# Position-table loads moved into the first block, and the first stage's seven-product block moved from fifth place to fourth

## The chip, the cores and the metric

The kernel runs on one core of one Trainium2 chip. The metric is the device time of one execution in microseconds (us), as the median of several runs. A profiled execution has, beside its time, a span: the stretch that the profiler's records cover.

## The reference

Two layers of a hybrid trunk work on one sequence of 256 tokens with 1024 channels, all in float32; a last RMSNorm follows. In each layer:

```
h = h + 1/2 * SwiGLU_a(RMSNorm(h))     # "ffn1": 1024 -> 2 x 2816 -> 1024
u = RMSNorm(h);  z = u @ W_in          # mixing: three causal branches (two attentions, one pooling)
h = h + m @ W_out
h = h + 1/2 * SwiGLU_b(RMSNorm(h))     # "ffn2", as ffn1

def swiglu(x, w_gate, w_up, w_down):
    return (silu(x @ w_gate) * (x @ w_up)) @ w_down
```

The attention branches need tables made from the input `positions` (256 integers): cosine and sine of rotary angles, and the negative distance between any two positions, masked causally. The differential attention also needs a scalar per layer worked out from the input `lamrow` (products, sums, exponentials). All of these are made once and used from the first mixing stage on.

## The kernel before

**Products.** Every float32 product is made of three matmuls on fp32r operands: a number is split into `hi`, a cast, and `lo`, the number less its cast, and `mm3` (L211 to L214) adds hi·hi (L212), lo·hi (L213, with the `lo` of the weights) and hi·lo (L214). Weights are split on the fly: a load on SyncE's queue (SP) brings a `raw` tile of 512 columns by 4 x 128 rows (1 MB; 6 buffers), ScalarE (ACT) casts `hi` (L194), VectorE (DVE) subtracts `lo` (L195); `hi` and `lo` have 3 buffers each. The first six tiles are loaded and split in four pieces of 128x512 (L200; 24 pieces of 256 KB in all).

**The opening.** After each of these pieces the list `opening` (filled at the end of the program, L1046 to L1052) gives up one callback. The callbacks load and split the columns of the transposed input, `u.first(k)` (L447 to L453: `uhi`, `ulo`), and then load the four quarters of `h`.

**A feed-forward stage**, `ffn` (L493 to L585), goes over the hidden width in blocks of 512 columns: c = 0, 512, 1024, 1536, 2048 and a last one of 256. A block makes the gate product (m=0) and the up product (m=1), each of two weight tiles and 48 matmuls. The results go through Silu (`sg`, ACT, L568) and a multiplication (`g`, DVE, L570). The `g` of a block is transposed during the next one, by `turned` (8 transposes, L503; split into `ghi` and `glo`, L486 and L487), behind the m=0 product or inside it. Block c=0 makes its four sums side by side. After each block `ahead` (L176) splits the next weight tile in advance.

**The seven-product block.** One block of a stage (`Seven`, L226 to L316) does its two products in seven half-size ones instead of eight. It needs prepared operands: `stream` (L236) makes sums and differences of the activations (`uf`, L240; `sf`, L245; `sh`, L249; `sl`, L250) two blocks ahead, and `sums` (L252) and `more` load the block's weight tiles (L161) and make differences of them (`t1`, `t2` and others, L258) one block ahead. Which block it is stands in `sevens` (L35 to L37): c=2048, the fifth, in layer 0's ffn1, and c=1536, the fourth, in the other three stages. The down projection (`Down`, L318 to L391) has similar preparations, made in block 2048, or in the last block where block 2048 is the seven-product one.

**The tables.** `tables` (L601 to L668) is called at the start of block c=512 of the first stage through `midway` (L515). It loads the positions twice, `pi` (two per partition, L607) and `pr` (all 256 to every partition, L608), and `lamrow` as `lr` (L658). All three loads are on ACT's queue. Before `pi` and `pr` stand copies on GpSimd (POOL) that write a bit of the block's `g` into the tiles, so that the loads don't start earlier. DVE then makes integer parts (`ci`, `ri`, L616), their floats (`cf`, `rf`, L618), distances (`part`, `ndist`, L620 to L625) and angles; ACT makes sines (L650 to L653) and exponentials (L663).

**What sets the order.** Each engine takes its instructions in order. The order on an engine is that of a scheduler working on the program as it is written; the times in the trace follow from semaphore waits. All loads on the two hardware queues share eight semaphores, DMAHW0 to DMAHW7, in rotation: a load waits until the load before it on its semaphore has landed.

Of the kernel before, what the change touches and what calls it, by code (L numbers as in the profile page):

```python
# [11 lines left out]
F32 = mybir.dt.float32  # L12
F32R = mybir.dt.float32r
I32 = mybir.dt.int32
# [5 lines left out]
P = 128  # L20
D = 1024
S = 256
DEPTH = 2
DFF = 2816
EPS = 1e-6
KD = D // P
# [5 lines left out]
NEG = -1e30  # L32


def sevens(layer, pre):  # L35

    return (2048,) if (layer, pre) == (0, "ffn1") else (1536,)  # L37

# [11 lines left out]
def plan():  # L52

    tiles = []

    def add(name, layer, k, nk, c, nc_):
        tiles.append((name, layer, k, nk, c, nc_))

    def ffn(layer, pre):
        for c in range(0, 2 * DFF, 1024):  # L60
            blocks = range(c, min(c + 1024, 2 * DFF), 512)
            order = [(b, k) for k in (0, 4) for b in blocks] if c == 0 else [(b, k) for b in blocks for k in (0, 4)]
            if c // 2 in sevens(layer, pre):
                order = [(c, 0), (c + 512, 0), (c + 512, 4), (c, 4)]
            for b, k in order:
                add(f"{pre}_gu", layer, k, 4, b, 512)
        for half in range(2):
            for k in range(0, KF, 4):
                add(f"{pre}_w_down", layer, k, min(4, KF - k), half * 512, 512)

    for l in range(DEPTH):
        ffn(l, "ffn1")
        for c, n in ((C_CQ, 416), (C_P, 512), (C_DQ, 512)):
            for k in (0, 4):
                add("w_in", l, k, 4, c, n)
        add("mla_w_uq", l, 0, 2, 0, 768)
        add("ukv", l, 0, 1, 0, 1024)
        for c in (C_DK, C_DV):
            for k in (0, 4):
                add("w_in", l, k, 4, c, 512)  # L80
        add("pool", l, 0, 4, 0, 128)
        for half in range(2):
            for i in range(3):
                for k in (0, 4):
                    add("w_in", l, k, 4, C_G + i * D + half * 512, 512)
        for half in range(2):
            for i in (2, 0, 1):
                add(f"w_branch{i}", l, 0, 4, half * 512, 512)
        for half in range(2):
            for k in (0, 4):  # L90
                add("w_out", l, k, 4, half * 512, 512)
        ffn(l, "ffn2")
    return tiles
# [3 lines left out]
def trunk(ctx, tc, x, xt, positions, wall, small, lamrow, fnorm, out):  # L97
    nc = tc.nc
# [8 lines left out]
    tp = ctx.enter_context(tc.tile_pool(name="tp", bufs=2))  # L107
    sp = ctx.enter_context(tc.tile_pool(name="sp", bufs=4))
# [10 lines left out]
    def big(shape, dt, name):  # L119
        return s8.tile(shape, dt, tag="s8", name=name, bufs=7)  # L120
# [44 lines left out]
    opening = []  # L165
# [4 lines left out]
    def wsplit(spec):  # L170

        if spec not in pending_splits:
            pending_splits[spec] = wsplit_now(spec)
        return pending_splits.pop(spec)
# [36 lines left out]
    def mm3(ps, lh, ll, rh, rl, start, stop):  # L211
        nc.tensor.matmul(ps, lhsT=lh, rhs=rh, start=start, stop=False)  # L212
        nc.tensor.matmul(ps, lhsT=lh, rhs=rl, start=False, stop=False)  # L213
        nc.tensor.matmul(ps, lhsT=ll, rhs=rh, start=False, stop=stop)  # L214
# [278 lines left out]
    def ffn(l, pre, u, following, midway=None):  # L493
        ghi, glo = [], []
# [18 lines left out]
        for c in range(0, DFF, 512):  # L513
            n = min(512, DFF - c)
            if c == 512 and midway:  # L515
                midway(g[0][:, :2])
            spec = lambda b, k: (f"{pre}_gu", l, k, 4, b, 512)
            if c == 0:

                ps = [[b() for _ in range(2)] for b in (acc, trp)]  # L520
                for k0 in (0, 4):
                    for m in range(2):
                        wh, wl = wsplit(spec(m * 512, k0))
                        for k in range(4):
                            for t in range(2):
                                tk = slice(t * P, (t + 1) * P)
                                mm3(ps[m][t], u.xh(k0 + k)[:, tk], u.xl(k0 + k)[:, tk], wh[:, k, :], wl[:, k, :],
                                    k0 + k == 0, k0 + k == KD - 1)
                if opened:
                    u.squares(0)  # L530
                    u.squares(1)
                u.factor()
                seven = Seven(u.xh, u.xl)
                down = Down(lambda k: ghi[0][:, k, :], lambda k: glo[0][:, k, :])
            elif c in sevens(l, pre):
                rows = seven.run(lambda: turned(*pending))
                ps = [[rows[t][m] for t in range(2)] for m in range(2)]
            elif n == 512:
                ps = []
                if c + 512 in sevens(l, pre):  # L540
                    at = 2 * c + 1024
                    last = latest[0]
                    seven.sums([spec(at, 0), spec(at + 512, 0), spec(at + 512, 4), spec(at, 4)])
                    latest[0] = last
                for m in range(2):
                    ps.append(gemm_tokens([spec(2 * c + m * 512, k) for k in (0, 4)], u.xh, u.xl, 512))
                    if m == 0:
                        turned(*pending)
                        if c + 1024 == sevens(l, pre)[0]:
                            seven.stream(u.hi, u.lo)  # L550
                        elif c == 2048 and c not in sevens(l, pre):
                            down.stream(ghi[0], glo[0], big)
            else:
                if not down.sh:
                    down.stream(ghi[0], glo[0], big)
                both = gemm_tokens([spec(2 * c, k) for k in (0, 4)], u.xh, u.xl, 512, lambda: turned(*pending))
                ps = [[b[:, m * n:(m + 1) * n] for b in both] for m in range(2)]
            if c + 512 in sevens(l, pre):
                seven.more()
            elif n < 512:  # L560
                down.open(lambda half, k: (f"{pre}_w_down", l, k, min(4, KF - k), half * 512, 512))
            elif c not in sevens(l, pre):
                ahead()
            g = []
            for t in range(2):
                r = u.r[:, t:t + 1]
                sg = tp.tile([P, n], F32, tag="B", name="sg")
                nc.scalar.activation(out=sg, in_=ps[0][t], func=AF.Silu, scale=r)  # L568
                gt = tp.tile([P, n], F32, tag="A", name="g", bufs=4)
                nc.vector.scalar_tensor_tensor(out=gt, in0=ps[1][t], scalar=r, in1=sg, op0=ALU.mult, op1=ALU.mult)  # L570
                g.append(gt)
            pending = c, g
# [25 lines left out]
    groups = [(0, range(p, NH, 2), P) for p in range(2)]  # L598
    groups += [(1, range(p + 4 * j, p + 4 * j + 4, 2), S) for j in range(2) for p in range(2)]

    def tables(after):  # L601
        pi = sp.tile([P, 2], I32, tag="pi", name="pi", bufs=1)
        pr = tp.tile([P, S], I32, tag="C", name="pr")

        nc.gpsimd.tensor_copy(out=pi, in_=after.bitcast(I32))
        nc.gpsimd.tensor_copy(out=pr[:, :2], in_=after.bitcast(I32))
        nc.scalar.dma_start(out=pi, in_=positions.rearrange("b (t p) -> (b p) t", p=P))  # L607
        nc.scalar.dma_start(out=pr, in_=positions.broadcast_to([P, S]))  # L608

        part = big([P, 2, 2, S], F32, "part")  # L610
        ci = sp.tile([P, 2, 2], I32, tag="ci", name="ci", bufs=1)
        cf = sp.tile([P, 2, 2], F32, tag="cf", name="cf", bufs=1)
        ri = tp.tile([P, 2, S], I32, tag="C", name="ri")
# [30 lines left out]
        for bits in (5, 13, 21, 40):  # L644
            c = math.floor(rest * 2.0 ** bits) / 2.0 ** bits if bits < 40 else rest
# [8 lines left out]
        nc.vector.tensor_scalar(out=sinq, in0=sink, scalar1=MLA_SCALE, scalar2=None, op0=ALU.mult)  # L654
        nc.vector.tensor_scalar(out=cosq, in0=cosk, scalar1=MLA_SCALE, scalar2=None, op0=ALU.mult)

        lr = tp.tile([P, DEPTH, 4, 32], F32, tag="C", name="lr")
        nc.scalar.dma_start(out=lr.rearrange("p l f d -> p (l f d)"), in_=lamrow.broadcast_to([P, DEPTH * P]))  # L658
        lpr = tp.tile([P, DEPTH, 2, 32], F32, tag="C", name="lpr")
        nc.vector.tensor_tensor(out=lpr, in0=lr[:, :, 0::2, :], in1=lr[:, :, 1::2, :], op=ALU.mult)  # L660
        le = sp.tile([P, DEPTH, 2], F32, tag="le", name="le", bufs=1)
# [360 lines left out]
    def last_half(n):  # L1022
# [8 lines left out]
        for t in range(2):  # L1031
# [4 lines left out]
            if n == 0:  # L1036
# [9 lines left out]
    u = Norm(0, SM_F1)  # L1046
    u.first(0)
    opening += [lambda: None] * 2 + [lambda: u.first(1), lambda: (u.first(2), u.first(3))]
    opening += [lambda k=k: u.first(k) for k in range(4, KD)] + [lambda: None] * 4
    opening += [lambda t=t, n=n: nc.sync.dma_start(out=h[:, t, n * 512:(n + 1) * 512],  # L1050
                                                   in_=x[t * P:(t + 1) * P, n * 512:(n + 1) * 512])
                for n in range(2) for t in range(2)]  # L1052
    for l in range(DEPTH):
        u = ffn(l, "ffn1", u, lambda: Norm(l, SM_MX), tables if l == 0 else None)
        u = mixing(l, u, lambda: Norm(l, SM_F2))
        u = ffn(l, "ffn2", u, (lambda: Norm(l + 1, SM_F1)) if l + 1 < DEPTH else None)
# [62 lines left out]
```

## Time and profile before

| | |
|---|---|
| median of 3 runs | 1215.74 us (1215.4 to 1217.15) |
| profiled execution | 1215.9 us |
| its span | 1214.1 us |
| mean granted TensorE clock | 0.993 |
| TensorE (PE) busy | 1189.3 us (98%), 5896 matmuls |
| PE waits for `lo` at L213, first 170 us | 8.9 us in 2, the longest 7.8 |

Times inside the profile are us from the span's start. A row of a timeline gives start, busy time, engine, line, operation, out<-in, and in brackets the idle time of the engine just before it with what ended it. "ACTq" and "SPq" are the issue of a load on ACT's or SP's queue. A granted clock of 1 is full speed. Matmuls are pipelined: one lasts 0.39 us in the records, and the next begins 0.23 us behind its start.

### The profile page before, as it was taken

To read this page: it belongs to the slowest core of one execution; us is meant where nothing else is said; L and a number is where in the kernel's file an instruction comes from. 1 tells how busy PE (TensorE), PEld (TensorE's weight loads), DVE (VectorE), ACT (ScalarE), POOL (GpSimd) and SP (SyncE) were. 2 spreads that over 40 slices of the span, in tenths; PEclk is the share of its full clock that TensorE was granted. 3 is DMA by queue.
4 is the path that set the end of the run, shared out by engine and by line. 5 is a ranking of instruction groups with operands and counts; after the bars stand their busy time and mean duration, and the time that the engine had idled before them with its cause. 6 is when DMAs were issued, how large, how long until landed. Compare 5 with 4: busy or idle time off the path is not lost.

```text
span 1214.1 us, 14983 instructions
## 1 busy us (share of the span) xinstructions
PE 1189.3 (98%) x5896; PEld 993.4 (82%) x5896; DVE 921.8 (76%) x1200; ACT 639.4 (53%) x817; POOL 65.8 (5%) x126
## 2 busy tenths in 40 slices
PE   9799899999999999999999999999999999999997
PEld 7688688998788888888888888899977888888886
DVE  6697977687766757997767997778677486499876
ACT  6446545455554454655464655455465535456543
POOL 0000000610100000000000000016000000000000
PEclk9899999999999999999999999999999999999999
DMA  9754346434445555463664463562443544545440
GB/s 320 280 180 152 133 167 231 148 139 174 139 139 177 195 175 170 153 244 112 231 243 171 146 243 118 211 217 83 168 143 137 208 173 174 184 165 206 163 166 35
DMA packets 35478, 212.86 MB, mean 175 GB/s; under 512 B 4176, under 2 KB 5584, under 8 KB 12112
## 3 DMA queue, kind: packets, MB, share of 16 engines
q1 hardware_dynamic: 34272, 210.52, 49.3%
q10 hardware_dynamic: 1136, 1.40, 0.4%
q8 instruction: 46, 0.75, 0.2%
q14 instruction: 24, 0.20, 0.0%
HBM read 210.85 MB, written 1.05 MB: 175 GB/s over the span
## 4 chain that ended last, share of the span: by engine, by line
PE 86%; DVE 6%; issue 3%; DMA 2%; ACT 2%; SPq 0%; POOL 0%; POOLq 0%; ACTq 0%; DVEq 0%
PE acc L212 17%; PE acc L213 17%; PE acc L214 17%; PE acc L278 11%; PE acc L344 10%; PE e L344 3%; PE o L853 2%; DVE lo L195 2%; PE tr L503 1%; PE tr L819 1%; PE tr L846 1%; DMA pr<-positions 1%; PE tr L213 1%; PE tr L212 1%; PE tr L214 1%
## 5 line engine op out<-in xcount | busy, mean ns | idle before, releaser
L195 DVE TENSOR_TENSOR lo<-raw,hi 128x1024 fp32r<-128x1024 f32 (+3 forms) x258 | 392.0, 1534 | 153.1 <-ACT hi L194 152.5
L194 ACT CAST hi<-raw 128x1024 fp32r<-128x1024 f32 (+3 forms) x258 | 328.7, 1297 | 276.2 <-PE acc L214 133.9
L213 PE MATMUL acc<-lo,uhi 128*128 128x512 f32 (+1 forms) x768 | 299.8, 390 | 8.9 <-DVE lo L195 8.9
L212 PE MATMUL acc<-hi,uhi 128*128 128x512 f32 (+1 forms) x768 | 301.0, 393 | 1.2 <-ACT hi L194 1.1
L214 PE MATMUL acc<-hi,ulo 128*128 128x512 f32 (+1 forms) x768 | 299.1, 390 | 0.4 <-DVE ulo L442 0.4
L213 PEld LDWEIGHTS acc<-lo,uhi 128*128 128x128 f32 x768 | 144.7, 188 | 38.4 <-DVE lo L195 9.9
L212 PEld LDWEIGHTS acc<-hi,uhi 128*128 128x128 f32 x768 | 144.2, 188 | 31.0 <-ACT hi L194 1.9
L214 PEld LDWEIGHTS acc<-hi,ulo 128*128 128x128 f32 x768 | 144.5, 188 | 30.2 <-DVE ulo L442 1.1
L222 ACT CAST hi<-raw 128x2048 fp32r<-128x2048 f32 x44 | 84.4, 1919 | 97.3 <-PE acc L214 32.8
L223 DVE TENSOR_TENSOR lo<-raw,hi 128x2048 fp32r<-128x2048 f32 x44 | 100.8, 2290 | 44.7 <-ACT hi L222 44.7
L838 ACT ACTIVATE e<-e,mx 128x128 f32<-128x128 f32 (+1 forms) x96 | 42.9, 449 | 55.9 <-DVE mx L834 34.1
L344 PE MATMUL acc<-hi,ghi 128*128 128x512 f32 x168 | 67.1, 399 | 1.6 <-ACT m L355 1.2
L344 PE MATMUL acc<-lo,ghi 128*128 128x512 f32 x168 | 67.1, 399 | 1.3 <-DVE lo L195 1.3
L344 PE MATMUL acc<-hi,glo 128*128 128x512 f32 x168 | 66.7, 398 | 0.0
L212 PE MATMUL acc<-uhi,hi 128*128 128x256 f32 x192 | 55.6, 290 | 0.0
L213 PE MATMUL acc<-ulo,hi 128*128 128x256 f32 x192 | 55.2, 288 | 0.0
L214 PE MATMUL acc<-uhi,lo 128*128 128x256 f32 x192 | 55.0, 288 | 0.0
L278 PE MATMUL acc<-hi,sh 128*128 128x512 f32 x128 | 49.9, 390 | 0.0
L278 PE MATMUL acc<-hi,sl 128*128 128x512 f32 x128 | 49.8, 389 | 0.0
L278 PE MATMUL acc<-lo,sh 128*128 128x512 f32 x128 | 49.8, 389 | 0.0
L417 POOL TENSOR_TENSOR r<-r,mhalf 128x2 f32<-128x2 f32 x6 | 4.2, 701 | 721.8 <-DVE r L416 721.8
L344 PEld LDWEIGHTS acc<-hi,ghi 128*128 128x128 f32 x168 | 32.1, 191 | 10.1 <-ACT m L355 2.3
(258 smaller groups left out, 1966.7 us busy)
## 6 DMA issues: line engine op xcount, KB each, us to landing
raw<-wall SPq DMA_DIRECT2D x182, 1024.0 KB, 4.9
raw<-wall SPq DMA_DIRECT2D x26, 256.0 KB, 5.2
raw<-wall SPq DMA_DIRECT2D x10, 512.0 KB, 3.5
raw<-wall SPq DMA_DIRECT2D x4, 832.0 KB, 4.3
raw<-wall SPq DMA_DIRECT2D x2, 768.0 KB, 6.6
xT<-xt SPq DMA_DIRECT2D x8, 128.0 KB, 4.5
h<-x SPq DMA_DIRECT2D x4, 256.0 KB, 6.5
fn<-fnorm ACTq DMA_DIRECT2D x1, 512.0 KB, 4.1
```

Source lines behind the costliest of these rows:

```text
L194: nc.scalar.copy(out=hif[:, ks], in_=rawf[:, ks])
L195: nc.vector.tensor_tensor(out=lof[:, ks], in0=rawf[:, ks], in1=hif[:, ks].bitcast(F32), op=ALU.subtract)
L212: nc.tensor.matmul(ps, lhsT=lh, rhs=rh, start=start, stop=False)
L213: nc.tensor.matmul(ps, lhsT=lh, rhs=rl, start=False, stop=False)
L214: nc.tensor.matmul(ps, lhsT=ll, rhs=rh, start=False, stop=stop)
L222: nc.scalar.copy(out=flat(hi), in_=flat(x))
L223: nc.vector.tensor_tensor(out=flat(lo), in0=flat(x), in1=flat(hi).bitcast(F32), op=ALU.subtract)
L278: nc.tensor.matmul(ps, lhsT=x, rhs=y, start=not onto and k == 0 and n == 0, stop=k == 3 and n == 2, skip_group_check=onto)
L344: nc.tensor.matmul(bank, lhsT=x, rhs=y, start=new and n == 0, stop=n == 2, skip_group_check=not new)
L503: nc.tensor.transpose(out=ptr[:, (i * 2 + t) * P:(i * 2 + t + 1) * P], in_=g[t][:, (j + i) * P:(j + i + 1) * P], identity=ident)
L838: nc.scalar.activation(out=e[:, sl], in_=e[:, sl], func=AF.Exp, bias=mx[:, i:i + 1], scale=-(2.0 ** -(hd + 1)) if slope else -1.0, accum_o ...
L853: nc.tensor.matmul(o[:, hd * 64:(hd + 1) * 64], lhsT=eT[:, j * P:(j + 1) * P], rhs=v[:, kt, hd * 64:(hd + 1) * 64], start=(kt == 0), stop= ...
```

## The change

The three table loads are taken out of `tables` into `table_loads`, which the opening calls behind the last `u.first`; the POOL copies in front of them now read the last column of `uhi`. Positions and `lamrow` land in a tile of their own, `tables`, which also holds `part`. `tables` itself stays where it was and computes from that tile. The seven-product block is at c=1536 in all four stages, which also changes the order of that stage's weights in memory (`plan`), and the fallback for the down projection's preparation goes.

```diff
-def sevens(layer, pre):
-    return (2048,) if (layer, pre) == (0, "ffn1") else (1536,)
+SEVEN = 1536
...
             if c == 512 and midway:
-                midway(g[0][:, :2])
+                midway()
...
-            elif c in sevens(l, pre):
+            elif c == SEVEN:
                 rows = seven.run(lambda: turned(*pending))
...
-                        if c + 1024 == sevens(l, pre)[0]:
+                        if c + 1024 == SEVEN:
                             seven.stream(u.hi, u.lo)
-                        elif c == 2048 and c not in sevens(l, pre):
+                        elif c == 2048:
                             down.stream(ghi[0], glo[0], big)
             else:
-                if not down.sh:
-                    down.stream(ghi[0], glo[0], big)
...
-    def tables(after):
-        pi = sp.tile([P, 2], I32, tag="pi", name="pi", bufs=1)
-        pr = tp.tile([P, S], I32, tag="C", name="pr")
-        nc.gpsimd.tensor_copy(out=pi, in_=after.bitcast(I32))
-        nc.gpsimd.tensor_copy(out=pr[:, :2], in_=after.bitcast(I32))
+    tb = {}
+    def table_loads(after):
+        tb["pi"] = pi = sp.tile([P, 2], I32, tag="pi", name="pi", bufs=1)
+        tb["all"] = big([P, 8, S], F32, "tables")
+        pr, lr = tb["all"][:, 4, :].bitcast(I32), tb["all"][:, 5, :]
+        for dst in (pi, pr[:, :2], lr[:, :2].bitcast(I32)):
+            nc.gpsimd.tensor_copy(out=dst, in_=after.bitcast(I32))
         nc.scalar.dma_start(out=pi, in_=positions.rearrange("b (t p) -> (b p) t", p=P))
         nc.scalar.dma_start(out=pr, in_=positions.broadcast_to([P, S]))
-        part = big([P, 2, 2, S], F32, "part")
+        nc.scalar.dma_start(out=lr, in_=lamrow.broadcast_to([P, DEPTH * P]))
+    def tables():
+        pi, pr = tb["pi"], tb["all"][:, 4, :].bitcast(I32)
+        part = tb["all"][:, 0:4, :].rearrange("p (t i) s -> p t i s", t=2)
...
-        lr = tp.tile([P, DEPTH, 4, 32], F32, tag="C", name="lr")
-        nc.scalar.dma_start(out=lr.rearrange("p l f d -> p (l f d)"), in_=lamrow.broadcast_to([P, DEPTH * P]))
+        lr = tb["all"][:, 5, :].rearrange("p (l f d) -> p l f d", l=DEPTH, f=4)
...
-    opening += [lambda k=k: u.first(k) for k in range(4, KD)] + [lambda: None] * 4
+    opening += [lambda k=k: u.first(k) for k in range(4, KD)]
+    opening += [lambda: table_loads(u.hi[:, KD - 1, :2].bitcast(F32))] + [lambda: None] * 3
```

Lines of the changed kernel are one lower than those of before up to the tables, and about three higher behind them. Three places of the new order matter. First, ACT's queue in block 1 and the start of block 2, before (casts of 128x512 are the pieces; `sg` are block 1's):

```order
L194 CAST hi<-raw 128x512 x13
L458 ACTIVATE sq,ss<-h 128x512
...
L568 ACT_TABLE_LOAD
L568 ACTIVATE sg<-acc,r 128x512
L194 CAST hi<-raw 128x512 x2
L568 ACTIVATE sg<-acc,r 128x512
L194 CAST hi<-raw 128x512 x5
L607 DMA pi<-positions 128x2x1
L608 DMA pr<-positions 128x256
L194 CAST hi<-raw 128x2048
L658 DMA lr<-lamrow 128x256
```

The same stretch of the changed kernel:

```order
L193 CAST hi<-raw 128x512 x10
L607 DMA pi<-positions 128x2x1
L608 DMA tables<-positions 128x256
L609 DMA tables<-lamrow 128x256
L193 CAST hi<-raw 128x512 x3
...
L654 ACT_TABLE_LOAD
L654 ACTIVATE sink<-ang 128x32
L655 ACTIVATE kk<-ang 128x32
L457 ACTIVATE sq,ss<-h 128x512
L193 CAST hi<-raw 128x512
L565 ACT_TABLE_LOAD
L565 ACTIVATE sg<-acc,r 128x512
```

The three loads moved from behind piece 24's cast to behind piece 10's, and the sine with a table load of its own now stands in front of piece 17's cast.

Second, SP's loads from piece 16 on with the semaphore that each waits for (`h` quarters among them), before:

```order
L200 DMA raw<-wall 128x512 [waits DMAHW3_49]
L1050 DMA h<-x 128x512 [waits DMAHW4_49]
L200 DMA raw<-wall 128x512 [waits DMAHW5_49]
L200 DMA raw<-wall 128x512 [waits DMAHW6_49]
L200 DMA raw<-wall 128x512 [waits DMAHW7_49]
```

and in the changed kernel:

```order
L199 DMA raw<-wall 128x512 [waits DMAHW6_49]
L1054 DMA h<-x 128x512 [waits DMAHW7_49]
L199 DMA raw<-wall 128x512 [waits DMAHW0_49]
L199 DMA raw<-wall 128x512 [waits DMAHW1_49]
L199 DMA raw<-wall 128x512 [waits DMAHW2_49]
```

The table loads take DMAHW6, 0 and 2, in that order, so the pieces 16, 17 and 19 now wait for a table load each, where they waited for an earlier load of SP's own.

Third, DVE in block 3 of the first stage (numbers tell tiles apart: lo_605 before, and lo_626 after, belong to the second weight tile of block 3's m=0 product, tile 10 in PE's order), before:

```order
L487 TENSOR_TENSOR glo_491<-tr_494,ghi_490 128x512
L240 TENSOR_TENSOR uf_647<-uhi_127,ulo_128 128x2048
L655 TENSOR_SCALAR cosq_119<-cosk_117 128x32
L245 TENSOR_TENSOR sf_649<-uf_647 128x512
L195 TENSOR_TENSOR lo_605<-raw_603,hi_604 128x2048
L570 SCALAR_TENSOR_TENSOR g_571<-acc_501,r_326,sg_569 128x512
```

and in the changed kernel:

```order
L486 TENSOR_TENSOR glo_490<-tr_493,ghi_489 128x512
L239 TENSOR_TENSOR uf_500<-uhi_127,ulo_128 128x2048
L244 TENSOR_TENSOR sf_502<-uf_500 128x512 x2
L244 TENSOR_TENSOR sf_502<-sf_502,uf_500 128x512
L567 SCALAR_TENSOR_TENSOR g_581<-acc_511,r_334,sg_579 128x512
L244 TENSOR_TENSOR sf_502<-uf_500,sf_502 128x512
L257 TENSOR_TENSOR t1_593<-raw_587,raw_589 128x2048
L249 TENSOR_TENSOR sl_508<-sf_502,sh_507 128x2048
L567 SCALAR_TENSOR_TENSOR g_585<-acc_512,r_334,sg_583 128x512
L257 TENSOR_TENSOR t2_594<-raw_591,t1_593 128x2048
L257 TENSOR_TENSOR raw_587<-raw_591,raw_587 128x2048
L194 TENSOR_TENSOR lo_626<-raw_624,hi_625 128x2048
```

The `lo` of tile 10 stood behind one `sf`; now it stands behind all four, behind `sl`, both `g` and the three weight differences.

More of the change, by code (lines that the diff above doesn't have):

```diff
@@ L62, in ffn @@
             order = [(b, k) for k in (0, 4) for b in blocks] if c == 0 else [(b, k) for b in blocks for k in (0, 4)]
-            if c // 2 in sevens(layer, pre):
+            if c // 2 == SEVEN:
                 order = [(c, 0), (c + 512, 0), (c + 512, 4), (c, 4)]
@@ L539, in ffn @@
                 ps = []
-                if c + 512 in sevens(l, pre):
+                if c + 512 == SEVEN:
                     at = 2 * c + 1024
@@ L548, in ffn @@
                         turned(*pending)
-                        if c + 1024 == sevens(l, pre)[0]:
+                        if c + 1024 == SEVEN:
                             seven.stream(u.hi, u.lo)
-                        elif c == 2048 and c not in sevens(l, pre):
+                        elif c == 2048:
                             down.stream(ghi[0], glo[0], big)
             else:
-                if not down.sh:
-                    down.stream(ghi[0], glo[0], big)
                 both = gemm_tokens([spec(2 * c, k) for k in (0, 4)], u.xh, u.xl, 512, lambda: turned(*pending))
                 ps = [[b[:, m * n:(m + 1) * n] for b in both] for m in range(2)]
-            if c + 512 in sevens(l, pre):
+            if c + 512 == SEVEN:
                 seven.more()
@@ L561, in ffn @@
                 down.open(lambda half, k: (f"{pre}_w_down", l, k, min(4, KF - k), half * 512, 512))
-            elif c not in sevens(l, pre):
+            elif c != SEVEN:
                 ahead()
```

## The prediction

> **What bounds the kernel now.** I read the page first, then windows over one feed-forward stage against its twin, then PE's waits, then the timelines of ACT and DVE around each wait. The page's head, and one row for each of two stages: layer 0's first FFN from the end of its block 1 to the first matmul of mixing, and layer 1's first FFN over the same stretch (length, then busy time of PE, PEld, DVE, ACT and POOL with instruction counts, then PE's granted clock, DMA share, GB/s).
>
> ```profile
> span 1214.1 us, 14983 instructions
> PE 1189.3 (98%) x5896; PEld 993.4 (82%) x5896; DVE 921.8 (76%) x1200; ACT 639.4 (53%) x817; POOL 65.8 (5%) x126
> 29.42:206.59 177.17, 164.46 (x726) 134.19 (x725) 140.76 (x135) 92.30 (x83) 1.39 (x4) 0.96 0.54 195
> 639.63:798.28 158.65, 158.65 (x726) 131.31 (x724) 132.69 (x98) 86.50 (x73) 0.00 (x0) 1.00 0.54 188
> ```
>
> TensorE is the bound. Layer 1's stage has no gap; layer 0's does the same 726 matmuls in 177.17 - 158.65 = **18.5 us** more: 177.17 - 164.46 = 12.7 idle, and 164.46 - 158.65 = 5.8 of slower matmuls at a mean clock of 0.96. That stage is what the change edits, so 18.5 is the most it can gain. The first part, in block 2, from the timelines of PE, ACT and DVE:
>
> ```profile
> 29.42 0.39 PE L212 MATMUL acc<-hi,uhi 128*128 128x512 f32 x1
> 40.30 1.04 PE L503 MATMUL tr<-ident,g 128*128 128x128 f32 x8
> 41.10 0.47 PE L212 MATMUL acc<-hi,uhi 128*128 128x512 f32 x1
> 49.41 0.79 PE L213 MATMUL acc<-lo,uhi 128*128 128x512 f32 x1 [7.84 <-DVE lo L195]
> ...
> 31.56 0.39 ACTq L607 DMA_DIRECT2D pi<-positions  x1
> 31.99 0.48 ACTq L608 DMA_DIRECT2D pr<-positions  x1
> 44.67 1.90 ACT L194 CAST hi<-raw 128x2048 fp32r<-128x2048 f32 x1 [10.16 <-DVE rf L618]
> ...
> 40.66 0.17 DVE L616 TENSOR_SCALAR ci<-pi 128x2 int32<-128x2 int32 x1 [7.51 <-DMA pi<-positions]
> 43.69 0.29 DVE L616 TENSOR_SCALAR ri<-pr 128x256 int32<-128x256 int32 x1 [2.32 <-DMA pr<-positions]
> 44.22 0.43 DVE L618 CAST rf<-ri 128x512 f32<-128x512 int32 x1
> 47.08 2.28 DVE L195 TENSOR_TENSOR lo<-raw,hi 128x2048 fp32r<-128x2048 f32 x1
> ```
>
> PE waits 7.84 us for the `lo` of tile 7 (tiles numbered in PE's order; 1 to 4 are block 1's, 5 to 8 block 2's, 9 to 12 block 3's). That `lo` starts at 47.08 because DVE, in order, had stood 7.51 and 2.32 us for the position loads; ACT stood 10.16 us in front of a cast, behind the issue of the third load. The second part, PE's waits between 100 and 185 us (total, times, longest), with the clock in three stretches:
>
> ```profile
> PE acc L344 <- DVE lo L195: 1.3, 1, 1.3
> PE acc L344 <- ACT m L355: 1.2, 1, 1.2
> PE acc L213 <- DVE lo L195: 1.1, 1, 1.1
> PE tr L503 <- DVE g L570: 0.9, 1, 0.9
> ...
> 52.00:53.00 1.00, 1.00 (x4) 0.75 (x4) 1.00 (x5) 0.05 (x1) 0.00 (x0) 0.72 1.04 442
> 148.00:150.00 2.00, 0.88 (x2) 0.78 (x3) 2.00 (x3) 0.42 (x1) 0.00 (x0) 0.53 0.00 0
> 154.00:156.00 2.00, 2.00 (x8) 1.64 (x7) 2.00 (x2) 0.00 (x0) 0.00 (x0) 0.76 0.39 78
> ```
>
> Four short waits, 4.5 us, fall where the seven-product block of this stage (fifth) runs straight into the last block and the down projection: there DVE is busy 2.00 of 2.00 us. If the clock is either 1 or a half, 0.53 puts its fall at 148.1 and 0.76 its return at 155.0: a piece of 6.8 us, 3.4 us lost in it. By 0.72 the clock came back at 52.6 after the first wait too, 3.1 us behind its end at 49.41, of which half is lost. So 7.8 and about 1.6 belong to the first part, about 9.1 to the second.
>
> **What goes: the second part.** With the seven-product block fourth, PE's order from there on is that of the other three stages, and layer 1's twin shows no wait in it: 9.1 us gained, less what new debt DVE carries in. **What goes: the first part.** The loads no longer stand in front of tile 7. They are issued behind the tenth cast on ACT's queue. That cast ends at 15.40 + 0.62 = 16.0 by the next row (three casts in 1.96 us), so the position column `pi` is issued at about 16.05; the three issues, 0.39 to 0.48 us each, push casts 11 to 13 to 17.4-19.3. PE works on tiles 1 to 3 until about 24 (29.42 less a tile's 5.44), so this costs nothing. Nor do the three small copies on POOL, which the page shows 5% busy, or the `tables` tile: it takes the buffer that `part` took in before, a block earlier, and no other tile asks for it then.
>
> ```profile
> 15.40 1.96 ACT L194 CAST hi<-raw 128x512 fp32r<-128x512 f32 x3 [0.78 <-DMA raw<-wall]
> lr<-lamrow ACTq DMA_DIRECT2D x1, 128.0 KB, 3.1
> sm<-small ACTq DMA_DIRECT2D x1, 82.0 KB, 2.6
> pi<-positions ACTq DMA_DIRECT2D x1, 1.0 KB, 9.1
> DMA to landing us min/median/max: 3.9/5.3/12.1
> q1 hardware_dynamic: 374, 2.68, 80.8%
> q10 hardware_dynamic: 367, 0.13, 7.0%
> q1 hardware_dynamic: 201, 0.36, 99.8%
> ```
>
> **What is added: two new waits.** These rows are the DMA issues of the first 60 us (KB, us to landing), the landing of `raw` tiles, and packets and MB of the queues at 36-44 us (q1 carries SP's loads, q10 ACT's) and at 16-17. In before `pi` took 9.1 us: its packets went in turn with SP's, 367 against 374, and SP's were 2.68 MB/374 = 7.2 KB each. At 16-17 they are 0.36/201 = 1.8 KB, a quarter. A nearly bare load takes 2.6 to 3.1; a quarter of the other 6.0 to 6.5 is 1.5 to 1.6; so 4.1 to 4.7, I take **4.4**: `pi` lands at 20.4. Bounds: 2.6 and 9.1. This matters because the loads take three turns in the rotation of eight DMA semaphores. SP's load of piece 16 now waits for the landing of `pi`, that of 17 for the second load's, that of 19 for the third's, and everything behind them on SP's queue waits too. Piece 16 is then issued at 20.4 and lands at 24.0: 3.6 us, between 3.1 for half its bytes and 3.9 for the quickest `raw`.
>
> From there ACT is a chain, priced by these rows:
>
> ```profile
> 23.24 0.64 ACT L458 ACTIVATE sq<-h 128x512 f32<-128x512 f32 x1
> 24.57 1.28 ACT L568 ACT_TABLE_LOAD   x1
> 25.87 0.69 ACT L568 ACTIVATE sg<-acc,r 128x512 f32<-128x512 f32 x1
> 52.95 0.23 ACT L650 ACTIVATE sink<-ang 128x32 f32<-128x32 f32 x1 [4.01 <-DVE ang L649]
> ...
> 30.54 1.41 DVE L570 SCALAR_TENSOR_TENSOR g<-tr,r,sg 128x512 f32<-128x512 f32 x2
> 31.86 1.28 DVE L195 TENSOR_TENSOR lo<-raw,hi 128x512 fp32r<-128x512 f32 x2
> 65.90 0.68 DVE L245 TENSOR_TENSOR sf<-uf,sf 128x512 f32<-128x512 f32 x1
> 73.10 2.28 DVE L195 TENSOR_TENSOR lo<-raw,hi 128x2048 fp32r<-128x2048 f32 x1
> 75.30 2.29 DVE L258 TENSOR_TENSOR t<-raw,t 128x2048 f32<-128x2048 f32 x1
> 77.51 1.28 DVE L487 TENSOR_TENSOR glo<-tr,ghi 128x512 fp32r<-128x512 f32 x2
> ```
>
> Five casts (16 to 20) 3.1, two table loads 2.6, sink and its neighbour 0.4, a square 0.7, two `sg` 1.3: 8.1, cast 20 ends near 32.1 and its `lo` at 32.7. By the table row the next activation starts 1.30 us after the load (24.57 to 25.87). The Trainium skill, "ScalarE: Activation LUTs", section "What ACT_TABLE_LOAD costs", adds a drain of about 1.38 us to a load of 1.28, 2.66 per switch; by it the chain and the sum would come out about 2.8 us higher. The row disagrees, and decides.
>
> DVE then follows its new order. Before the last four `lo` of block 2's first product stand a small one 0.1, two `g` 1.3 (30.54 to 31.86), `rf` 0.4, small ones 0.2, and the distances, 47.08 - 44.65 = 2.4: it reaches them at 37.1, the first ends at 37.7. PE needs it half a product, 5.44, behind 29.42 and one matmul more, at 35.1: **wait 2.6**. The four end at 39.5; two whole `lo` at 2.2 (73.10 to 75.30) 43.9; the third waits for its cast, whose buffer PE frees at 37.7 + 5.3 = 43.0, so 43.0 + 1.9 + 2.2 = 47.1. Then `glo` 1.2, `uf` 2.2, three `sf` 1.8, `g` 0.7, `sf` 0.6, t1 2.2, `sl` 2.2, `g` 0.7, t2 2.2, one more difference 2.2: 63.1, and only then tile 10's `lo`, **65.2**. Unhindered, PE asks for it at 29.42 + 10.88 (a product, 29.42 to 40.30) + 0.8 (transposes, to 41.10) + 10.88 + 5.44 + 0.45 + 0.8 + 0.45 = 59.1. Both waits together are thus **6.1**: 2.6 and 3.5. In before that `lo` stood ahead of the differences; here the sums of the seven-product block come a block earlier and pass it.
>
> **The clock.** It fell within the 7.84 us wait, and again at 148.1 where no wait exceeds 1.3. So I count one piece of 6.8 us after the second wait, 3.4 lost less some 0.2 inside the wait: **3.2**; bounds 0 and twice that, nearer one piece. The three bounds together (landing 2.6: two us less; clock 0) give the low end.
>
> **Sum.** 1215.9 for the profiled execution, - 18.5 + 6.1 + 3.2 = 1206.7; the median of the runs shown is 0.16 below that execution, so **1206.5**.
>
> **The rivals.** *The clock stays up*: 1206.5 - 3.2 = **1203.3**. For it: neither wait comes near 7.84 unbroken. Against it: the fall at 148.1 came with shorter ones. The Trainium skill, "TensorE: Matmul & The Clock Gate", section "HAM oscillation — how this bites in real kernels", asks for an idle gap above some 3.4 us; by that the clock would hardly fall here, and the trace at 148 us disagrees with it. Chance 0.27; the forecast itself, with the clock lowered once, 0.45.
> *A landing as in before*, 9.1 us: everything behind piece 16 is 4.7 later, **1211.2**; the queue was as busy at 16 us as at 36 (99.8%), but its packets are shorter; 0.12.
> *No new wait*: loads land in 2.6 and the buffers give DVE slack, all 18.5 gained, **1197.4**; against it stands the `lo` behind five whole-tile operations; 0.06.
> *The fourth block stalls as the fifth did*, DVE coming into it with its debt: the 9.1 of the second part isn't gained, **1215.6**, no change; the twin stage speaks against it; 0.05.
> *Slower*: the tiny packets of `pi` delay SP's queue so long that pieces 16 to 24 become the bound. It decides once `pi` lands over 16 us behind its issue (4.4 + 11.6, where 1206.7 passes 1218.3); at 18 us it gives **1220**. The longest landing above is 12.1; 0.05.
>
> **How the numbers follow.** A measurement of this kernel tells about 0.2%, 2.4 us, from no change. Below 1213.3 lie the forecast, the clock that stays, the late landing and the clean stage: 0.45 + 0.27 + 0.12 + 0.06 = 0.90; same 0.05, slower 0.05. The range goes from 1201.0 (clock up, quick landing) to 1212.0, which leaves out the clean stage, the last two rivals and a third of the late landing: 0.20.
>
> **What would show it.** The first landing near 20.4, piece 16 near 24; no 7.8 us wait at tile 7, but 2.6 near 35 and 3.5 near 62, both for DVE's `lo`; one half-clock piece behind the second; no PE gap between 110 and 160; the stretch from block 1's end to mixing about 168 us. I am wrong if pieces 16 to 24 land as early as before, if DVE has tile 10's `lo` before 60, or if gaps remain at the down projection.

## The result and the profile after

The changed kernel takes **1207.36 us** (median of 4 runs, 1206.68 to 1208.36) against 1215.88 (1215.40 to 1217.15) of the kernel before on the same chip: ratio 0.9929, 95% interval 0.9912 to 0.9946, so 0.5 to 0.9% faster. The forecast was 1206.5. The profiled execution took 1207.28 us with a span of 1205.5: 8.6 less than before's profiled one, which is what the next rows have to account for.

First the changed stage and its middle, in windows (columns as before): from the end of block 1, now at 29.70, to the first matmul of mixing, and the 50 us in which the kernel before had its short waits.

```profile
29.70:197.81 168.11, 161.83 (x726) 132.06 (x724) 141.13 (x120) 94.42 (x87) 1.37 (x3) 0.99 0.58 213
110.00:160.00 50.00, 50.00 (x230) 41.22 (x230) 42.17 (x30) 28.21 (x24) 0.00 (x0) 1.00 0.42 152
```

The stage has come down from 177.17 to 168.11 us; the clean twin took 158.65. Of the 9.5 us that are left, 168.11 - 161.83 = 6.3 are idle. In the second row PE is busy all of 50.00 us at full clock: the second part of the old excess is gone. The idle time stands in three rows of PE's timeline:

```profile
32.31 0.50 PE L212 MATMUL acc<-lo,uhi 128*128 128x512 f32 x1 [0.23 <-DVE lo L194]
...
39.00 0.50 PE L212 MATMUL acc<-lo,uhi 128*128 128x512 f32 x1 [2.31 <-DVE lo L194]
...
46.02 1.03 PE L502 MATMUL tr<-ident,g 128*128 128x128 f32 x8
...
64.49 0.71 PE L211 MATMUL acc<-hi,uhi 128*128 128x512 f32 x2
68.89 0.50 PE L212 MATMUL acc<-lo,uhi 128*128 128x512 f32 x1 [3.69 <-DVE lo L194]
```

0.23 at tile 5, 2.31 at tile 6, 3.69 at tile 10: 6.23. The loads and what stands behind them, from the issues of the first 60 us and the timelines of ACT, SP and DVE:

```profile
pi<-positions ACTq DMA_DIRECT2D x1, 1.0 KB, 4.2
...
16.35 0.39 ACTq L607 DMA_DIRECT2D pi<-positions  x1
25.62 0.62 ACT L193 CAST hi<-raw 128x512 fp32r<-128x512 f32 x1 [0.34 <-DMA raw<-wall]
32.53 0.62 ACT L193 CAST hi<-raw 128x512 fp32r<-128x512 f32 x1
46.22 1.91 ACT L193 CAST hi<-raw 128x2048 fp32r<-128x2048 f32 x1 [2.04 <-PE acc L213]
...
20.60 0.33 SPq L199 DMA_DIRECT2D raw<-wall  x1
...
20.61 0.17 DVE L620 TENSOR_SCALAR ci<-pi 128x2 int32<-128x2 int32 x1 [0.26 <-DMA pi<-positions]
35.20 0.42 DVE L622 CAST rf<-ri 128x512 f32<-128x512 int32 x1
37.85 0.49 DVE L629 SCALAR_TENSOR_TENSOR ndist<-tables 128x256 f32<-128x256 f32 x1
38.27 7.09 DVE L194 TENSOR_TENSOR lo<-raw,hi 128x512 fp32r<-128x512 f32 x6
64.35 2.29 DVE L257 TENSOR_TENSOR raw<-raw 128x2048 f32<-128x2048 f32 x1
66.55 2.28 DVE L194 TENSOR_TENSOR lo<-raw,hi 128x2048 fp32r<-128x2048 f32 x1
```

`pi` is issued at 16.35 and takes 4.2 us; SP issues piece 16 at 20.60, right behind its landing, and ACT casts it at 25.62. Cast 20 starts at 32.53. From 35.20 to 38.27 DVE works out the distances, with a few rows of 0.2 us among them, and only then it reaches block 2's last four pieces; PE had asked for the first of them at 36.69 (39.00 - 2.31). For block 3, ACT's cast at 46.22 waited for PE, which had just done with tile 6 (46.02). Tile 10's `lo` starts at 66.55, behind the third difference.

### The profile page after: what moved, and what is told of

It reads as the page before. It is cut to its first block, busy times and chain, and to the rows that moved or that the text cites. A ratio compares the mean times of both kernels' runs of the same rounds, so it can differ in the third digit from the quotient of the medians.

```text
span 1205.5 us, 14989 instructions
## 1 busy us (share of the span) xinstructions
PE 1186.7 (98%) x5896; PEld 991.4 (82%) x5896; DVE 923.0 (77%) x1200; ACT 637.7 (53%) x817; POOL 66.2 (5%) x127
## 4 chain that ended last, share of the span: by engine, by line
PE 88%; DVE 6%; issue 2%; ACT 2%; DMA 2%; POOL 0%; SPq 0%; POOLq 0%; ACTq 0%; DVEq 0%
PE acc L211 17%; PE acc L212 17%; PE acc L213 17%; PE acc L277 13%; PE acc L343 9%; PE e L343 3%; PE o L856 2%; DVE lo L194 2%; PE tr L502 1%; DMA raw<-wall 1%; PE tr L822 1%; PE tr L849 1%; PE tr L212 1%; PE tr L213 1%; PE tr L211 1%
## 5 line engine op out<-in xcount | busy, mean ns | idle before, releaser
L565 ACT ACTIVATE sg<-acc,r 128x512 f32<-128x512 f32 (+1 forms) x44 | 28.5, 653 | 27.7 <-PE acc L213 27.7
```

## The experiments

In each, PE's waits are quoted from its timeline or its list of waits (total, times, longest). The theories' letters are those of the expectations.

### The two halves of the change, each alone

The first kernel has the early loads and the `tables` tile, and keeps the old places of the seven-product block:

```diff
 def sevens(layer, pre):
     return (2048,) if (layer, pre) == (0, "ffn1") else (1536,)
...
+    opening += [lambda: table_loads(u.hi[:, KD - 1, :2].bitcast(F32))] + [lambda: None] * 3
```

> The early table loads alone; the first stage's seven-product block stays fifth. Theory A (two independent debts: the loads' place sets the waits of block 2, the seven-product block's place sets the stall at 130 to 155 us): the 7.8 us wait and its half clock (9.4 us together) go, the changed kernel's own waits in block 2 come (1.1 + 2.3, and 1.7 of half clock, 0.3 of a later block 1), and the short waits between 130 and 155 us with their half-clock piece stay: 1215.9 - 9.4 + 5.4 = about 1212. Rival B (one debt: DVE comes late to the fifth block because of the tables): the stall at 130 to 155 us goes too, about 1203.

It took 1210.09 us, against 1215.76 of the kernel before in the same comparison (0.9955, 0.9940 to 0.9969). Its PE waits behind 30 us:

```profile
PE acc L213 <- DVE lo L195: 3.8, 4, 2.3
PE acc L344 <- DVE lo L195: 1.3, 1, 1.3
PE acc L344 <- ACT m L355: 1.2, 1, 1.2
```

The first row holds the 2.3 of tile 6, as in the changed kernel. The others are the same waits, to a tenth, that the kernel before had at the down projection. Rival B is out: the fifth-place stall doesn't depend on the tables. The time is 2 us under the expectation, and the clock gives more than that: in the profiled execution it isn't lowered in block 2, and at 144 a half-clock piece lasts 3.4 us instead of 6.8, so that 1.7 us less is lost at each place.

The second kernel has the block fourth and the old loads:

```diff
+SEVEN = 1536
...
-    opening += [lambda: table_loads(u.hi[:, KD - 1, :2].bitcast(F32))] + [lambda: None] * 3
+    opening += [lambda: None] * 4
```

> The seven-product block fourth alone; the table loads stay in block 2. Theory A: the 7.8 us wait for tile 7 stays; the stall at 130 to 155 us goes (9.1 us); DVE's new order in block 3 brings a wait for tile 10's lo of about 5 us (adding the same operations up from tile 7's lo: DVE there at about 73.8, PE at 68.8): 1215.9 - 9.1 + 5.0 = about 1212, up to 1215 if the clock falls after it. Rival B: tile 10's wait in the changed kernel is owed to the late pieces 16 to 24, which land here as in before; then it is missing and the time is about 1207.

1214.37 us (0.9988, 0.9979 to 0.9998). PE's timeline:

```profile
50.83 0.80 PE L212 MATMUL acc<-lo,uhi 128*128 128x512 f32 x1 [8.78 <-DVE lo L194]
75.40 0.80 PE L212 MATMUL acc<-lo,uhi 128*128 128x512 f32 x1 [4.67 <-DVE lo L194]
```

The wait for the loads is there, a little longer, and tile 10's wait is there with 4.67 where 5.0 was worked out, though no piece is late here. Moving the block alone is worth 0.1%: what it saves at the down projection it gives back in block 3 and in the longer wait for the loads. The clock is lowered twice, as in the kernel before, and for as long in all (10.24 and 3.41 us here, 6.83 twice before).

### Who makes tile 10's wait

The third kernel is the changed one with the three loads at the very start of ACT's queue:

```diff
-        for dst in (pi, pr[:, :2], lr[:, :2].bitcast(I32)):
-            nc.gpsimd.tensor_copy(out=dst, in_=after.bitcast(I32))
...
+    table_loads()
     u = Norm(0, SM_F1)
     u.first(0)
```

> The changed kernel with the three table loads at the very start of ACT's queue, without the copies on POOL before them; no load of SP waits for their semaphores later. Theory A: pieces 16 to 24 land as in before (22.5 to 28.8, all later by at most 0.8 for 0.26 MB more at the start); the waits for tiles 5 and 6 shrink from 3.4 to under 0.8, no half clock there, and tile 10's wait stays at 3.5 to 3.7, since its chain begins when PE frees a buffer after tile 6: 1207.3 - 1.1 - 2.3 - 1.7 + 1.2 = about 1203.4. Rival B (tile 10's wait is the late pieces' debt): it goes as well, about 1199.7. Rival C (the late pieces aren't owed to the semaphores but to the packets of the table loads, or the start suffers): 1206 or more.

1205.91 us (0.9916, 0.9899 to 0.9932). PE's waits, and DVE at the start:

```profile
PE acc L211 <- DVE ang L649: 2.2, 1, 2.2
...
37.60 0.50 PE L212 MATMUL acc<-lo,uhi 128*128 128x512 f32 x1 [0.60 <-DVE lo L194]
65.93 0.79 PE L212 MATMUL acc<-lo,uhi 128*128 128x512 f32 x1 [3.69 <-DVE lo L194]
...
5.76 0.17 DVE L618 TENSOR_SCALAR ci<-pi 128x2 int32<-128x2 int32 x1 [0.49 <-DMA pi<-positions]
33.80 0.41 DVE L620 CAST rf<-ri 128x512 f32<-128x512 int32 x1
```

Tile 6's wait shrank to 0.60, and tile 10's stayed at 3.69, the same number as in the changed kernel: A holds, B is out. The distances still stand ahead of block 2's last pieces here, but DVE starts on them at 33.80 instead of 35.20. The time is 2.5 above A's expectation, and two things stand behind it: DVE now works out the first angles at 5.76, ahead of `uhi`, for which PE waits 2.2 in the opening; and the clock was lowered twice.

The fourth kernel leaves the loads as in the changed one and writes the three differences behind the m=0 product, in the first stage only:

```diff
+        def subs(self):
             sub = lambda o, x, y: nc.vector.tensor_tensor(out=flat(o), in0=flat(x), in1=flat(y), op=ALU.subtract)
...
                         turned(*pending)
+                        if c + 512 == SEVEN and ((l, pre) == (0, "ffn1")):
+                            seven.subs()
```

> The changed kernel with the three weight differences of the first stage's seven-product block written behind block 3's m=0 product instead of ahead of it; by the order, two of them now follow tile 10's lo on DVE. Theory A (the order makes tile 10's wait): that lo ends 4.4 us earlier, the wait of 3.7 goes to 0, waits for tiles 5 and 6 stay: 1207.3 - 3.7 = about 1203.6. Rival D (DVE is short of time in block 3 altogether, whatever its order): the wait moves to tile 11, 12 or the fourth block, about 1207.

1203.72 us (0.9897, 0.9882 to 0.9912), within 0.2 of A by the median; its four runs lie between 1202.13 and 1204.86. Its waits behind 30 us:

```profile
PE acc L212 <- DVE lo L194: 2.5, 2, 2.3
PE acc L280 <- ACT hi L221: 1.4, 1, 1.4
```

Tile 10's wait is gone, tile 6's is unchanged, and 1.4 of it comes back at the start of the seven-product block, where D had a wait come back. The rest of tile 10's wait doesn't return anywhere, so D fails for the greater part: DVE had most of the time, and did things in the wrong order.

### Who makes tile 6's wait

My account was that the pieces come late because SP waits for the table loads' semaphores. The next kernel takes the loads off those semaphores by issuing them from POOL's queue:

```diff
-        nc.scalar.dma_start(out=pi, in_=positions.rearrange("b (t p) -> (b p) t", p=P))
+        nc.gpsimd.dma_start(out=pi, in_=positions.rearrange("b (t p) -> (b p) t", p=P))
```

(and the other two likewise).

> The changed kernel with its three table loads at the same place, behind the last column of uhi, but issued from POOL's queue, which by the order takes no turn in the eight semaphores that SP's loads use. Theory S (pieces 16 to 24 are late because SP waits for the landing of the table loads): pieces 16 to 24 land within 0.5 us of before (22.5 to 28.8), tile 5's loss of 1.1 and tile 6's wait of 2.3 with its half clock of 1.7 shrink to under 0.8 together, tile 10's wait stays 3.7: 1207.3 - 5.1 + 0.8 = about 1203.0, up to 1204.7 if the clock falls at tile 10. Rival P (the small packets of the table loads slow SP's transfers themselves): pieces 16 to 24 stay late, about 1207.

1208.43 us (0.9938, 0.9921 to 0.9955): no better than the changed kernel. The runs spread from 1205.72 to 1210.86, and the profiled one is the slowest of them. SP's issue of the 24 pieces (times of one, then first and last start) in the kernel before, in the changed kernel,

```profile
L200 SPq DMA_DIRECT2D raw<-wall x24: 327/430/1263, 1.2 to 23.5; - x24
```

```profile
L199 SPq DMA_DIRECT2D raw<-wall x24: 328/430/1073, 1.2 to 27.2; - x24
```

and in this one, with PE's waits and ACT's row at the sine:

```profile
L199 SPq DMA_DIRECT2D raw<-wall x24: 327/393/794, 1.2 to 22.6; - x24
...
40.13 0.50 PE L212 MATMUL acc<-lo,uhi 128*128 128x512 f32 x1 [2.23 <-DVE lo L194]
70.07 0.80 PE L212 MATMUL acc<-lo,uhi 128*128 128x512 f32 x1 [3.69 <-DVE lo L194]
...
27.51 0.23 ACT L654 ACTIVATE sink<-ang 128x32 f32<-128x32 f32 x1 [5.13 <-DVE ang L653]
...
36.33 0.42 DVE L622 CAST rf<-ri 128x512 f32<-128x512 int32 x1
```

The last piece is issued at 22.6, as early as in the kernel before, where the changed one had 27.2: the semaphores did hold SP up. But tile 6 waits as long as ever. With the pieces in time, ACT stood 5.13 us in front of them for the sine's input, which waits for `pi` (5.6 us on this queue), and DVE came to the distances at 36.33, later than in the changed kernel. So late pieces, which S and P both call for, aren't needed for tile 6's wait; here late positions had taken their place. That gave theory W: it is that DVE and ACT stand for the table loads and work out the tables, put by the order ahead of the casts and the `lo` of block 2, that costs PE the time.

Two more kernels had POOL's queue and a later place for the sums: the first with only the differences behind the m=0 product, the second with the three tile loads moved too.

```diff
                     if m == 0:
                         turned(*pending)
+                        if c + 512 == SEVEN and ((l, pre) == (0, "ffn1")):
+                            at = 2 * c + 1024
...
+                            seven.sums([spec(at, 0), spec(at + 512, 0), spec(at + 512, 4), spec(at, 4)])
```

> Both remedies at once: table loads from POOL's queue, and the first stage's weight differences written behind block 3's m=0 product. Theories A and S together: no wait over 0.8 us in blocks 1 and 2, none at tile 10, at most the 1.4 us at the start of the seven-product block seen with the later differences alone: 1203.0 - 3.7 + 0.4 = about 1199.7. Rival D (DVE short of time altogether): waits come back in blocks 3 and 4, 1202 or more.

> As the kernel before it, but the loads of the three weight tiles are written behind the m=0 product too, so that tile 10's lo stands ahead of all three differences and of sl. Theory A: no wait at tile 10; the price is that the seven-product block's tiles load and are split later, so the 1.4 us at its start may grow: about 1199.7, between 1199 and 1202.

1205.67 us (0.9915, 0.9900 to 0.9930) and 1203.46 (0.9892, 0.9876 to 0.9908): 4 to 6 us over the expectations. Tile 6's wait remains in both, 2.04 in the first and 2.23 in the second, against the 0.8 that A and S together allowed, and tile 10's is absent in both. The runs of the first spread from 1202.8 to 1208.1, and the profiled one is its fastest, so its median isn't explained by its profile.

To test W, the tables' operations are held back to the fifth block, by copies on POOL that also read that block's `g`:

```diff
-            if c == 512 and midway:
-                midway()
+            if c == 2048 and midway:
+                midway(g[0][:, :2])
...
+        pi = sp.tile([P, 2], I32, tag="pi2", name="pi2", bufs=1)
+        nc.gpsimd.tensor_copy(out=pi, in_=after.bitcast(I32))
+        nc.gpsimd.tensor_copy(out=pi, in_=tb["pi"])
```

> The changed kernel with the loads on POOL's queue and the tables worked out in the fifth block instead of at the start of the second: copies on POOL that also read that block's g hold the column of positions and the lamrow values back until then. The sums of the seven-product block stay as in the changed kernel. Theory W (what costs PE its waits at tiles 5 and 6 is that DVE and ACT stand for the table loads and work out the tables there, wherever the loads are issued): no wait over 0.6 us before tile 10. Theory A: tile 10's wait stays at 3.7, as its chain begins when PE has done tile 6. Together 1215.9 - 18.5 + 3.7 = about 1201.1, up to 1203 with the clock. Rival D (the tables' 5 us of DVE work and two or three table loads of ACT are paid in the fifth and sixth block instead): 1204 or more, with waits after 120 us.

1206.56 us (0.9930, 0.9914 to 0.9947). PE's waits behind 30 us that exceed 0.5 us:

```profile
63.57 0.59 PE L212 MATMUL acc<-lo,uhi 128*128 128x512 f32 x1 [3.69 <-DVE lo L194]
...
113.73 0.51 PE L211 MATMUL acc<-hi,uhi 128*128 128x512 f32 x1 [0.66 <-ACT hi L193]
116.37 0.50 PE L212 MATMUL acc<-lo,uhi 128*128 128x512 f32 x1 [2.14 <-DVE lo L194]
```

Blocks 1 and 2 run without a wait over 0.25 us behind 30 us: W holds there. Tile 10's 3.69 is there for the fourth time. And D holds in part: the same operations now cost 0.66 and 2.14 in the fifth block, where DVE has just as little room. The time is 5.5 above 1201.1; these 2.8 and 1.7 for a half-clock piece behind tile 10's wait make up 4.5 of it.

With the sums moved as well:

> As the kernel before it, and the sums of the first stage's seven-product block written behind block 3's m=0 product, loads and differences. Theories W and A: no wait over 0.6 us from block 2 to mixing, the clean stage of 158.7 us: 1215.9 - 18.5 = about 1197.4, up to 1199 for what the fifth block pays. Rival D: 1201 or more, with waits after 120 us.

1202.53 us (0.9889, 0.9874 to 0.9904); D again, through the fifth block's two waits alone, 0.66 and 2.14 as in the kernel before it, now ending at 108.15 and 110.79.

Last, the tables in the last block (`c == 2560` in the line above), once with the loads on POOL's queue, once on ACT's. The second kernel also calls the loads eight callbacks later, behind the `h` quarters; ACT issues them from 16.23 to 17.77, between casts 10 and 13.

```diff
-    opening += [lambda: table_loads(u.hi[:, KD - 1, :2].bitcast(F32))] + [lambda: None] * 3
+    opening += [lambda: None] * 4
...
+    opening += [lambda: table_loads(u.hi[:, KD - 1, :2].bitcast(F32))]
```

> As the last kernel (table loads on POOL's queue, sums behind the m=0 product), but the tables are worked out in the last, half-size block instead of the fifth. DVE was busy 14.1 us of 20 at 140 to 160 us in the changed kernel, against 18.1 at 120 to 140, so there is room for some 5 us. Theory W: the two waits at the fifth block, 0.7 and 2.1, go and none comes: 1202.5 - 2.8 = about 1199.7. Rival D: waits of 2 us or more in the last block or the down projection, 1202 or more.

> As the kernel before it, but with the table loads on ACT's queue as in the changed kernel; by the order, SP's pieces 16, 17 and 19 again wait for their semaphores, while no engine stands for the loads or works out tables before the last block. It has the semaphores' price by itself. Theory S: pieces 16 to 24 land about 2 us and more later than in before, and PE waits 2 us at tiles 5 and 6: 1201.7 or more. Theory W: the late pieces alone cost PE nothing, since tile 6's first lo is needed only at 35.1: within 0.7 of the kernel before it, about 1199.7.

1202.43 us (0.9885, 0.9870 to 0.9900) and **1201.34** (0.9877, 0.9860 to 0.9893; runs from 1201.27 to 1201.45). The first has two waits, again where the tables' operations now stand, so D holds for it too:

```profile
PE acc L343 <- ACT m L354: 1.9, 1, 1.9
PE e L343 <- ACT hi L193: 0.7, 1, 0.7
```

The second has late pieces without the tables' operations. Its stage in windows, and from the timelines of SP, ACT and PE:

```profile
29.64:191.93 162.29, 160.15 (x724) 131.83 (x723) 142.58 (x136) 93.37 (x87) 2.02 (x6) 0.99 0.60 220
```

```profile
20.14 0.33 SPq L199 DMA_DIRECT2D raw<-wall  x1
...
20.99 5.96 SPq L199 DMA_DIRECT2D raw<-wall  x8
...
30.79 3.00 ACT L193 CAST hi<-raw 128x512 fp32r<-128x512 f32 x5
...
134.04 0.50 PE L343 MATMUL acc<-hi,ghi 128*128 128x512 f32 x1 [1.90 <-ACT m L354]
```

SP issues piece 16 at 20.14 and the last one near 26, almost as late as the changed kernel's 20.60 and 27.2 and over 2 us behind the 23.5 of the kernel before. ACT, with nothing of the tables before it, has cast the last five pieces by 33.8, where the changed kernel had just cast piece 20. PE meets no wait over 0.25 us between 30 and 134. Late pieces alone cost nothing, as W says: S fails as the cause of tile 6's wait by itself. The 1.90 at 134 is D's once more, where the tables' operations stand. This kernel has the lowest median of all, 0.5% under the changed one by the medians of their own comparisons, but its interval overlaps those of the two before it; its stage is 162.29 us long, 3.6 above the clean twin.

What the runs leave open for the changed kernel is how the 2.31 divides. Without the tables' operations in block 2 there is no wait. With them it lasts 0.60 where the loads come first and neither pieces nor positions are late, 2.23 where only the positions are late, and 2.31 where the pieces are. No run of the changed kernel's order has the pieces and the positions in time together with the opening undisturbed.

## Why the prediction was right

**What goes.** Both parts of the old 18.5 us went as stated: no 7.8 us wait at tile 7, no gap at the down projection. The kernels with one half each show that the parts are separate.

**The loads.** `pi` was to be issued at 16.05, take 4.4 us and land at 20.4; it was issued at 16.35 and took 4.2, and DVE used it at 20.61. Pricing a load by a bare one plus the packets that it takes turns with gave the number within 0.2 us; two other kernels with this load on ACT's queue at that place had 4.6 and 3.9. That the turns make the price was not tested by itself.

**Piece 16** is where the chain was off. It was to land at 24.0; its cast started at 25.62. I gave it 3.6 us, between a load of half its bytes and the quickest `raw`, and it took about 5.0 (20.60 to 25.62). So cast 20 ended a good 1 us later than stated (32.1 against 32.53 + 0.62), and DVE reached the four pieces at 38.27 instead of 37.1. PE was later too, block 1 ending at 29.70 and tile 5 being late, so the wait came out at 2.31 instead of 2.6, with 0.23 ahead of it that I hadn't counted.

**Tile 6's cause.** The size was right and the reason incomplete. I let the chain start from pieces held up by semaphores. The last experiment has the pieces nearly as late and no wait; the one with POOL's queue has the pieces in time and the wait of 2.23. What the changed kernel and the one with POOL's queue share is what the prediction added up behind the pieces: two table loads on ACT, the sine, and the distances on DVE, all ahead of block 2's last pieces. The sum came out because it ran through those operations: by DVE's rows the distances alone take 35.20 to 38.27, and a `lo` in their place would have ended near 35.9, before PE asked at 36.69. The lateness matters too, as the wait of 0.60 with the loads first shows, but only on top of them.

**Tile 10.** 3.5 was stated and 3.69 measured, and the chain was the right one, though its times weren't: the `lo` ended at 68.83 instead of 65.2, and PE asked 3.5 us later as well. The prediction had the link that explains this, the buffer that PE frees at the end of tile 6: it put it at 43.0, and it came at 46.02 (the transposes' row). From there to the end of the `lo` it took 22.8 us (22.2 in the prediction), against 19.2 (18.7) that PE needs to ask for it (46.02 to 65.2). The wait is the difference, so its size doesn't depend on the wait before it, which the prediction's sum up to a fixed 65.2 doesn't say: it is 3.69 in four kernels with tile 6's wait at 2.31, 0.60, 2.23 and nothing. That holds while the chain starts at PE; with the old loads DVE was behind from tile 7's `lo` on, and the wait was 4.67. The order made it, as stated, and the kernel with later differences took it away.

**The clock.** This term was mis-sized: 3.2 for one piece of 6.8 us behind tile 10's wait; measured was one piece of 3.4 us behind tile 6's, 1.7 lost (the section at the end), and none behind tile 10's. So the place was wrong as well as the size, and the section at the end shows that with the same wait for tile 10 the clock did fall in three other kernels. This is one execution: its mean granted clock was 0.998, and those of the other three runs 0.997, 0.996 and 0.996. The rival with the clock up, 1203.3, is out too. In the sum the 1.5 too much was made up by 1.5 us of matmuls that the view counts as busy (161.83 - 158.65 - 1.7), most of them late starts at tile 5 and beside the waits, and 0.3 came from the later end of block 1: -18.5 + 6.2 + 1.7 + 1.5 + 0.3 = -8.8, and -8.6 was measured. The forecast was 0.9 us off the median, with errors of 1 to 2 us in its terms that cancelled, and that is luck.

**The other rivals.** A landing as in before is refuted by the 4.2 us. No new wait and a fourth block that stalls are refuted by PE's rows; slower, by the landing.

## What to carry to other kernels

A load that is issued early helps only as far as the engines' order lets it: find out what the scheduler now puts ahead of the critical casts, and hold that work back to a place with room, by a dependency if it must be. A wait at the end of a chain that starts from the waiting engine itself doesn't grow or shrink with the waits before it, so follow a chain to its start before summing. Here a side work of some 6.7 us on DVE (its rows for the tables in the changed kernel) was moved through a stage in which DVE is 84% busy (141.13 of 168.11 us), and each place cost 2 to 3 us of waits: try two or three places, not one.

## What the runs showed of the hardware

The granted clock changed on a grid with a step of 3.41 us: a piece at half clock lasted one step in the changed kernel and two in the kernel before, whose two falls, at 45.73 and 148.13, lie 102.40 us or thirty steps apart. These are windows of one step each: for the changed kernel the step before the fall, the piece itself, and the two steps of tile 10's wait; for the kernel before the steps ahead of its two falls.

```profile
36.33:39.75 3.42, 1.11 (x5) 0.49 (x3) 3.42 (x11) 3.42 (x4) 1.32 (x2) 1.00 1.02 429
39.75:43.16 3.41, 3.41 (x9) 2.68 (x9) 3.41 (x4) 2.00 (x2) 0.00 (x0) 0.50 1.01 423
63.64:67.05 3.41, 1.56 (x11) 1.06 (x9) 3.41 (x3) 2.72 (x3) 0.00 (x0) 1.00 0.00 0
67.05:70.47 3.42, 1.58 (x7) 1.32 (x8) 3.42 (x4) 0.00 (x0) 0.00 (x0) 1.00 0.22 34
```

```profile
42.32:45.73 3.41, 0.00 (x0) 0.00 (x0) 2.04 (x9) 1.06 (x1) 0.00 (x0) 1.00 0.25 96
144.72:148.13 3.41, 1.76 (x7) 0.96 (x7) 3.41 (x4) 2.49 (x3) 0.00 (x0) 1.00 0.02 5
```

A wait of 2.31 us within one step, PE busy 1.11, was followed by a fall; a longer one, 3.69, that lay across two steps, 1.56 and 1.58 busy, was not. With the same 3.69 the clock did fall, inside the wait or within 0.3 us behind it, in the kernels with the loads first, with POOL's queue and with the tables in the fifth block, whose steps before the fall were:

```profile
62.24:65.65 3.41, 0.00 (x1) 0.00 (x0) 3.41 (x2) 2.00 (x2) 0.00 (x0) 1.00 0.00 0
```

```profile
65.07:68.48 3.41, 1.31 (x10) 0.88 (x8) 3.41 (x3) 2.47 (x3) 0.00 (x0) 1.00 0.00 0
```

```profile
60.42:63.84 3.42, 0.27 (x1) 0.27 (x2) 3.42 (x3) 0.62 (x2) 0.00 (x0) 1.00 0.00 0
```

So what counts is how the wait lies on the grid, not its length alone. The other kernels fit a limit near half of a step, with PE busy by the windows before a fall or without one: fallen in the kernel with the early loads alone and in the last one,

```profile
140.78:144.20 3.42, 1.47 (x7) 0.78 (x6) 3.42 (x4) 2.04 (x2) 0.00 (x0) 1.00 0.02 5
```

```profile
131.11:134.52 3.41, 1.51 (x8) 0.94 (x6) 3.41 (x7) 3.41 (x8) 0.00 (x0) 1.00 0.00 0
```

and not fallen in the one with POOL's queue and later differences:

```profile
36.35:39.76 3.41, 1.82 (x7) 1.34 (x8) 3.41 (x9) 3.39 (x3) 1.31 (x2) 1.00 1.01 423
```

But 1.76 fell and 1.56 did not, so the limit isn't settled by these rows. The Trainium skill, "TensorE: Matmul & The Clock Gate", section "What's actually happening", speaks of a free-running window of about 3.4 us: the grid agrees with that. Its section "HAM oscillation — how this bites in real kernels" asks for an idle gap above some 3.4 us, and here the measurements decide otherwise, in both directions: a gap of 2.31 was enough, and one of 3.69 was not always.
